# A third pair of key tiles in the second attention, and a norm's broadcast two projection steps later

## The chip, the cores and the metric

The kernel runs on one core of one Trainium2 chip. The metric is the device time of one execution in microseconds (us). The kernel before takes 2125.5 us in the median of three runs (2124.99 to 2128.76). A profiled execution, with the start and end of every instruction on each engine, took 2126.15 us.

The engines are named as in the profile: PE is TensorE (matmuls), PEld its weight loads, DVE is VectorE, ACT is ScalarE, POOL is GpSimd, SP is SyncE, which here only starts DMAs. Every engine works through its own instructions in a fixed order; an instruction waits until what it needs is done, and everything behind it on the same engine waits with it.

## What is computed

A trunk of two layers over 1024 tokens of width 1024, all in float32. Each layer is a token mixer with an attention of 12 heads (64 wide), beside it 4 heads that attend to 256 fixed memory tokens, then an output projection and a SwiGLU. Layer 0 mixes by windowed attention, layer 1 by attention over a neighbourhood on a grid.

```python
for i in range(DEPTH):                       # 2 layers
    h = rmsnorm(x, norm_mix[i])
    mk, mv = split(mem_n @ w_mem_kv[i])
    if i % 2 == 0:
        q, k, v, qm = split(h @ w_in_a)      # 12 query heads, 4 key/value heads
        y_tok = windowed_gqa(q, k, v, sink)
    else:
        q, k, v, qm = split(h @ w_in_b)      # 12 query, 12 key, 12 value heads
        y_tok = neighbourhood_attn(q, k, v, rpb)
    y_mem = memory_attn(qm, mk, mv)          # 4 heads
    x = x + concat([y_tok, y_mem]) @ w_out[i]
    h = rmsnorm(x, norm_ffn[i])
    x = x + (silu(h @ w_gate) * (h @ w_up)) @ w_down[i]
return rmsnorm(x, norm_final)
```

## The kernel before

Everything lies transposed, features on the 128 partitions and tokens along a row, in two column halves of 512 tokens (f = 0 and 1). To keep float32 accuracy, every operand is split into a high and a low part, and a product is three matmuls: high by high, high by low, low by high. A projection of 128 output features over one half is a sum of 8 steps (the 8 tiles of 128 input features) of 3 matmuls each, 24 matmuls of 128x512, named `mm`.

The split of a weight tile is a cast on ACT (the high part, line 106) and a subtraction on DVE or POOL (the low part, line 109). The tiles are `wf` for the first three units of a layer, then `wqk`, `wv` and `wqm` for units that make query and key, value, and memory query. Weights come by DMA from the queue of SP.

**The change of layers** is `first_dense`. While the down projection of layer 0 ends, it starts the three first units of layer 1 (24 matmuls each) on the first half, whose norm is done. Between the steps it pushes along the norm of the second half: squares, sums by matmul (`st`, line 213), a power of -1/2 (`nv` on DVE, `nr` on POOL), a diagonal matrix (`diag` on DVE, line 237), and a matmul with ones (`bc`, line 249) that spreads the factors over all partitions. Then eight times a scaling on DVE, a cast on ACT and a subtraction on DVE make the tiles `hT` of the second half, which the same three units need next. `Norm.split` has a number `lag`: so many calls pass between the diagonal and `bc`.

**The attention of a layer** (20 units and 16 heads in layer 1) runs units and heads at the same time. A head is worked in two halves of four query blocks. For each block a score product `S` (two matmuls, with the high and low part of the keys, KH and KL), the softmax on DVE, ACT and POOL, and per half the transposes of the four probability blocks `pT`, their split into `ph` and `pl`, and the products with the values, `O`. The heads' order is two memory heads, heads 0 to 5, the two other memory heads, heads 6 to 11. While a head's matmuls are put down, steps of the projections of later units are drawn in between (`pull`), as many as are due.

A unit `qk` of layer 1 makes the query tile `QS` of a head and its key tiles `KH` and `KL`. High parts of the keys are written by ACT and low parts by DVE straight out of the projection's PSUM bank, and two DMAs of SP (line 656) copy them to the other 64 partitions. The keys of a memory head (`mKH`, `mKL`, one pair for two heads) lie in tiles of the same ring. Before, the ring of layer 1 has 2 pairs and that of queries 3 tiles:

```python
nq = 4 if is_a else 3
Q[h] = k4("QS", nq, "QS")
K[i] = k4("KH", 2, "KH"), k4("KL", 2, "KL")
mk = k4("KH", 2, "mKH"), k4("KL", 2, "mKL")
```

The order in which each engine's instructions stand is not that of the code. A scheduler orders them when the program is built, by priority (the code's order) and by when an operand or a free tile is expected; a write to a ring that is full is put behind the last reader of the oldest tile. So the numbers of tiles and the address of each tile set the order and the waits. The tiles of a pool reuse the memory of the pools before it and wait for the last use there.

Of the kernel before, what the change touches and what calls it, by code (L numbers as in the profile page):

```python
# [41 lines left out]
def trunk_kernel(ctx: ExitStack, tc: tile.TileContext, a: dict, out: bass.AP):  # L42
# [68 lines left out]
    def load_w(src, tag="whl", bufs=3, eng=None, name="w", pool=wp, parts=1, raw=None):  # L111
        if raw is None:
            raw = raw_tile(f"{name}_raw")
            nc.sync.dma_start(raw, src)
        w = pool.tile([P, 2, D], F32R, tag=tag, name=name, bufs=bufs)
        for i in range(parts):
            c = slice(i * D // parts, (i + 1) * D // parts)
            hi(w[:, 0, c], raw[:, c])
            pieces = 4 if eng is nc.gpsimd else 1
            for j in range(pieces):  # L120
                n = D // parts // pieces
                cj = slice(i * D // parts + j * n, i * D // parts + (j + 1) * n)
                lo(w[:, 1, cj], raw[:, cj], w[:, 0, cj], eng)
        return w
# [9 lines left out]
    def steps(ps, w, h, order=range(NK), n=HS, start=True, stop=True):  # L134

        order = list(order)
        for i, k in enumerate(order):
            terms = three(wk(w, k), (h[k][:, 0, :n], h[k][:, 1, :n]))
            for j, (l, r) in enumerate(terms):
                nc.tensor.matmul(  # L140
                    ps[:, :n], l, r, start=start and i == 0 and j == 0,
                    stop=stop and i == len(order) - 1 and j == 2,
                )
            yield

    def run(g):
        for _ in g:
            pass
# [5 lines left out]
    def first_dense(layer, norm):  # L154

        pre = []
        src = a["w_in_b"]
        todo = (norm.add(x[k][1]) for k in range(len(norm.xs), NK))
        parts = norm.split(layer, hT[1], 6)
        for n, u in enumerate(FIRST[layer]):  # L160
            w = load_w(src[u], eng=nc.gpsimd, name="wf")
            wide[:] = True, (4, 2, 3)[n]
            ps = mm_tile()
            for i, _ in enumerate(steps(ps, w, hT[0])):
                if next(todo, 0) is not None and (n or i > 3):
                    next(parts, None)
            pre.append((w, ps))
        run(parts)
        return pre

    def mm_tile(name="mm"):

        wide[1] += 1
        if wide[0] and wide[1] % 5 > 2:
            return ps_s.tile([P, HS], F32, tag="S", name=name)
        if wide[0] and wide[1] % 5 == 0:
            return ps_t.tile([P, HS], F32, tag="T", name=name)
        return ps_mm.tile([P, HS], F32, tag="mm", name=name)
# [108 lines left out]
    with tc.tile_pool(name="mp", bufs=1, reuse_waits="tile") as mp:  # L287
# [60 lines left out]
        hT = [[None] * NK, [None] * NK]  # L348
# [12 lines left out]
        def total(norm, parts, n=D):  # L361

            both = []
            for t in parts:
                sq = mp.tile([P, D], F32, tag="sq", name="sq", bufs=2) if n == D else temp("sq")
                nc.scalar.activation(sq, t, AF.Square)
                both.append(sq)
                if len(both) > 1:
                    nc.vector.tensor_tensor(both[0], both[0], both.pop(), op=ALU.add)
                yield  # L370
            t = both[0]
            while n > norm.n:
                n //= 2
                nc.vector.tensor_tensor(t[:, :n], t[:, :n], t[:, n : 2 * n], op=ALU.add)
            norm.acc = [t[:, :n]]
            yield
# [8 lines left out]
        parts = total(norms[0], [xp[k, 0] for k in range(0, NK, 2)])  # L385
# [78 lines left out]
        for i in range(8):  # L464
# [11 lines left out]
            if i == 0:  # L476
                nc.scalar.copy(unit_scale, norms[0].scale())
                norms[1].xs = {k: x[k][1] for k in range(NK)}
                parts = total(norms[1], [xp[k, 1] for k in range(0, NK, 2)])
# [40 lines left out]
    for layer in range(2):  # L520
        is_a = layer == 0
        with tc.tile_pool(name=f"ap{layer}", bufs=1, reuse_waits="tile") as ap:
# [2 lines left out]
            wi = a["w_in_a"] if is_a else a["w_in_b"]  # L525
            n_tok = 10 if is_a else 18
            n_v = 8 if is_a else NH
            nq = 4 if is_a else 3


            def seen(ps):
# [6 lines left out]
            def placed(t, f):  # L538
                if is_a:
                    return t.rearrange("p (r f c) -> p f r c", f=2, c=32)[:, f]  # L540
                return t[:, f * HS : (f + 1) * HS].rearrange("p (s r c) -> p r s c", s=4, c=SC)

            def k4(tag, bufs, name):
                return ap.tile([P, S], F32R, tag=tag, bufs=bufs, name=name)

            def put_q(dst, f, ps, odd, order=True):

                rs = slice(HD, P) if odd else slice(0, HD)
                ot = slice(0, HD) if odd else slice(HD, P)
                if order:  # L550
                    src, h, l = seen(ps[rs]), placed(dst[rs], f), placed(dst[ot], f)
                    hi(h, src)
                    lo(l, src, h)
                else:
                    src, h, l = ps[rs], dst[rs, f * HS : (f + 1) * HS], dst[ot, f * HS : (f + 1) * HS]
                    nc.scalar.mul(h, src, SCALE)
                    nc.vector.scalar_tensor_tensor(
                        l, src, SCALE, h.bitcast(F32), op0=ALU.mult, op1=ALU.subtract
                    )

            def put_k(kh, kl, f, ps):
                rs = slice(HD, P)
                src, h, l = seen(ps[rs]), placed(kh[rs], f), placed(kl[rs], f)
                hi(h, src)
                lo(l, src, h)
# [14 lines left out]
            Q, K, V = {}, {}, {}  # L580

            class Unit:
# [21 lines left out]
                def open(self):  # L604
                    i = self.i
                    if self.kind == "qk":
                        h = 3 * i if is_a else i
                        Q[h] = k4("QS", nq, "QS")
                        K[i] = k4("KH", 2, "KH"), k4("KL", 2, "KL")
                        self.put = lambda f, ps: (put_q(Q[h], f, ps, False), put_k(*K[i], f, ps))  # L610
                    elif self.kind == "v":
                        V[2 * i], V[2 * i + 1] = (
                            ap.tile([P, 8, 2, HD], F32R, tag="V", bufs=4, name="V") for _ in range(2)
                        )
                        self.vt = ap.tile([P, S], F32, tag="vT", bufs=1, name="vT")
                        self.put = lambda f, ps: nc.scalar.copy(placed(self.vt, f), seen(ps))
                    else:
                        mem = self.kind == "qm"
                        hs = [("m", 2 * i), ("m", 2 * i + 1)] if mem else [3 * i + 1, 3 * i + 2]
                        for h in hs:  # L620
                            Q[h] = k4("QS", nq, "QS")
                        if mem:
                            mk = k4("KH", 2, "mKH"), k4("KL", 2, "mKL")
                            mv = ap.tile([P, 8, 2, HD], F32R, tag="V", bufs=4, name="mV")
                            K["m", i], V["m", i] = mk, mv
                            for j in range(2):
                                src = memk_d[layer, j][:, i * NM : (i + 1) * NM].rearrange(
                                    "(i p) k -> p i k", i=2
                                )
                                for rs in (slice(0, HD), slice(HD, P)):  # L630
                                    nc.sync.dma_start(
                                        mk[j][rs, :HS].rearrange("p (i k) -> p i k", i=2).bitcast(F32), src
                                    )
                            nc.sync.dma_start(
                                mv[:, :4].rearrange("p (b m) i d -> p b m (i d)", b=2).bitcast(F32),
                                memv_d[layer].rearrange("p (b m e) -> p b m e", b=2, m=NMH)[
                                    :, :, 2 * i : 2 * i + 2
                                ],
                            )
                        self.put = lambda f, ps: [  # L640
                            put_q(Q[h], f, ps, j == 1, order=not mem) for j, h in enumerate(hs)
                        ]
# [344 lines left out]
        with (  # L987
# [241 lines left out]
            for f in range(2):  # L1229
                for m in range(NK):  # L1230
# [15 lines left out]
                    if f == 1 and m == 0:  # L1246
                        norms[0].sums()
                        parts = norms[0].raw(2 + layer)
# [328 lines left out]
            parts = iter(())  # L1577
            hT = [[None] * NK, [None] * NK]
            for at_, (i, g) in enumerate(dorder):
# [28 lines left out]
                if i == 6 and g > 0:  # L1608
                    if g == 1:
                        parts = norms[0].split(1, hT[0], 1) if is_a else finish(norms[0])  # L1610
# [9 lines left out]
            if is_a:  # L1620
                pre = first_dense(1, norms[1])
            else:
                run(end)
                run(finish_end(quarter[1]))
# [88 lines left out]
```

## Time and profile before

| | before |
|---|---|
| median of three runs | 2125.5 us |
| profiled execution, its own time | 2126.15 us |
| span from first to last instruction | 2124.1 us |
| granted TensorE clock, mean | 0.998 |
| change of layers (first units of layer 1) | from about 1017 us |
| second attention | about 1066 to 1396 us |

A profile's time is that of one execution; the span lies between its first and last instruction, and 2.05 us lie around it. A row of a timeline has start, duration, engine, line, operation, output and input tiles, shape and count, and in square brackets the engine's idle time ahead of it with what ended it. The chain of waits follows the work that ended last back from the end: its rows have start, duration, engine, tile and line. In the timelines fp32 matmuls that take two passes (`st`, `bc`) count twice.

### The profile page before, as it was taken

The numbers are of one execution on the slowest core, as the hardware profiler recorded it, in microseconds if no ns is written. First come the engines' busy times: TensorE is split into PE (matmuls) and PEld (weight loads), VectorE is DVE, ScalarE is ACT, GpSimd is POOL, SyncE is SP. The second block draws the span as 40 slices with busy tenths as digits, with TensorE's granted clock in tenths as the row PEclk, the third lists the DMA queues.
The fourth block names the chain that finished last, engine by engine and source line by source line (L and its number), as shares of the span: only waits on it lengthen the run. The fifth ranks groups of instructions, "written<-read, shape, count | busy, mean of one in ns | idle before, by whom it ended". The sixth has DMA issues, their size and how long they took to land.

```text
span 2124.1 us, 29029 instructions
## 1 busy us (share of the span) xinstructions
PE 2094.9 (99%) x10316; PEld 1749.5 (82%) x10316; DVE 1521.0 (72%) x2477; ACT 1066.8 (50%) x2035; POOL 576.0 (27%) x614
## 2 busy tenths in 40 slices
PE   9999999999999999999999999999999999999998
PEld 7788888888888888888778888888788888888886
DVE  7687887787666666866765666667986666677675
ACT  6687775444434335344465666654443434344442
POOL 0344330234444430000233233203243444410000
PEclk9999999999999999999999999999999999999999
DMA  6421128332333227866232222275232323277662
GB/s 231 145 82 50 31 94 275 98 113 101 110 114 108 87 104 256 312 219 205 74 95 81 69 65 69 79 257 159 73 111 105 109 102 107 99 252 254 205 223 87
DMA packets 120913, 287.28 MB, mean 135 GB/s; under 512 B 12224, under 2 KB 20672, under 8 KB 120768
## 3 DMA queue, kind: packets, MB, share of 16 engines
q1 hardware_dynamic: 112880, 271.63, 37.9%
q10 hardware_dynamic: 7888, 13.79, 1.7%
q8 instruction: 82, 1.34, 0.3%
q14 instruction: 63, 0.52, 0.1%
HBM read 210.40 MB, written 68.94 MB: 132 GB/s over the span
## 4 chain that ended last, share of the span: by engine, by line
PE 90%; DVE 4%; ACT 2%; issue 1%; DMA 1%; POOL 1%; ACTq 0%; DVEq 0%; SPq 0%; POOLq 0%
PE X L1078 16%; PE Y L1078 16%; PE mm L140 15%; PE X L1509 11%; PE Y L1509 8%; PE po L140 8%; PE O L786 3%; PE S L723 3%; PE pT L766 3%; PE X L1160 2%; PE Y L1160 2%; PE mm L426 1%; DMA wd_kept<-in_w_dn 1%; DVE pl L109 0%; PE bc L249 0%
## 5 line engine op out<-in xcount | busy, mean ns | idle before, releaser
L1078 PE MATMUL Y<-hB,wgu 128*128 128x512 f32 x1056 | 255.6, 391 | 0.8 <-ACT c L1098 0.8
L1078 PE MATMUL X<-hB,wgu 128*128 128x512 f32 x1056 | 255.0, 391 | 0.0
L1509 PE MATMUL X<-hB,wd 128*128 128x512 f32 (+1 forms) x1092 | 243.8, 383 | 0.9 <-DVE x L1473 0.9
L109 DVE TENSOR_TENSOR wgu<-wS,wgu 128x1024 fp32r<-128x1024 f32 (+1 forms) x124 | 152.9, 1233 | 121.7 <-ACT wgu L106 121.6
L1509 PEld LDWEIGHTS X<-hB,wd 128*128 128x128 f32 x1092 | 200.1, 188 | 41.9 <-issue 2.2
L1078 PEld LDWEIGHTS Y<-hB,wgu 128*128 128x128 f32 x1056 | 196.7, 188 | 43.4 <-ACT c L1098 1.6
L1078 PEld LDWEIGHTS X<-hB,wgu 128*128 128x128 f32 x1056 | 195.8, 188 | 40.2 <-ACT g L1095 0.4
L751 POOL TENSOR_SCALAR p<-p,stat 128x384 f32<-128x384 f32 (+1 forms) x256 | 139.3, 563 | 317.7 <-DVE stat L748 223.1
L140 PE MATMUL mm<-hT,wqk 128*128 128x512 f32 x672 | 197.5, 404 | 1.5 <-DVE KL L109 1.5
L106 ACT CAST wgu<-wS 128x1024 fp32r<-128x1024 f32 (+1 forms) x124 | 114.2, 923 | 149.9 <-POOL wS L1035 124.5
L140 PE MATMUL po<-yT,wo 128*128 128x512 f32 x768 | 185.6, 394 | 0.0
L1509 PE MATMUL Y<-hB,wd 128*128 128x512 f32 x792 | 180.7, 389 | 0.1
L1509 PEld LDWEIGHTS Y<-hB,wd 128*128 128x128 f32 x792 | 148.5, 188 | 31.7 <-DVE x L1473 0.5
L234 POOL TENSOR_TENSOR nr<-nv,neg_half 128x4 f32<-128x4 f32 (+1 forms) x12 | 13.4, 1116 | 586.0 <-DVE nv L233 582.1
L140 PEld LDWEIGHTS po<-yT,wo 128*128 128x128 f32 x768 | 142.5, 188 | 29.9 <-issue 1.0
L1078 PE MATMUL X<-hT,wgu 128*128 128x512 f32 x624 | 150.2, 391 | 0.0
L106 ACT CAST hB<-b_raw 128x512 fp32r<-128x512 f32 x154 | 89.5, 618 | 113.5 <-DMA b_raw<-b_d 94.5
L1035 POOL TENSOR_TENSOR wS<-wgu_raw 128x512 f32<-128x512 f32 x44 | 60.9, 1384 | 294.6 <-DVE wgu L109 294.6
L1078 PEld LDWEIGHTS X<-hT,wgu 128*128 128x128 f32 x624 | 117.0, 188 | 26.2
L738 ACT ACTIVATE p<-p,stat 128x256 f32<-128x256 f32 (+1 forms) x192 | 112.5, 587 | 51.5 <-DVE stat L734 49.5
L109 DVE TENSOR_TENSOR pl<-pT,ph 128x384 fp32r<-128x384 f32 (+1 forms) x256 | 118.5, 492 | 18.4 <-ACT ph L106 15.3
L109 DVE TENSOR_TENSOR hB<-b_raw,hB 128x512 fp32r<-128x512 f32 x154 | 99.8, 686 | 42.8 <-ACT hB L106 42.4
(208 smaller groups left out, 4230.6 us busy)
## 6 DMA issues: line engine op xcount, KB each, us to landing
wgu_raw<-in_w_gu SPq DMA_DIRECT2D x92, 512.0 KB
wd_raw<-in_w_dn SPq DMA_DIRECT2D x70, 512.0 KB
b_raw<-b_d SPq DMA_DIRECT2D x70, 512.0 KB
b_d<-c SPq DMA_DIRECT2D x88, 256.0 KB
b_d<-t SPq DMA_DIRECT2D x66, 256.0 KB
wo_raw<-in_w_out SPq DMA_DIRECT2D x32, 512.0 KB
xr_d<-x ACTq DMA_DIRECT2D x32, 256.0 KB
xr<-xr_d SPq DMA_DIRECT2D x16, 512.0 KB
```

The source lines that it names most:

```text
L106: nc.scalar.copy(dst, src)
L109: (eng or nc.vector).tensor_tensor(dst, src, h.bitcast(F32), op=ALU.subtract)
L140: nc.tensor.matmul(ps[:, :n], l, r, start=start and i == 0 and j == 0, stop=stop and i == len(order) - 1 and j == 2,)
L723: nc.tensor.matmul(s_[:, :n], Q[self.h][:, qb * P : (qb + 1) * P], k, start=j == 0, stop=j == 1)
L738: nc.scalar.activation(p[:, :n], p[:, :n], AF.Exp, bias=m1, scale=-1.0, accum_out=s1)
L751: nc.gpsimd.tensor_scalar(p[:, :n], p[:, :n], ri[:, i : i + 1], 1.0, op0=ALU.mult, op1=ALU.mult)
L766: nc.tensor.transpose(tr[:, j * P : (j + 1) * P], p[:, j * P : (j + 1) * P], ident)
L786: nc.tensor.matmul(o[:, c0 : c0 + w * P], self.value(j), t[:, s0 : s0 + w].rearrange("p j q -> p (j q)"), start=j == js[0] and t is self.p ...
L1035: sub = lambda o, p_, q_: nc.gpsimd.tensor_tensor(o, p_, q_, op=ALU.subtract)
L1078: nc.tensor.matmul(ps, l, r, start=n in (0, 1, 3, 6) and k == 0 and i == 0, stop=k == 3 and i == 2, skip_group_check=True,)
L1160: nc.tensor.matmul(bank[:, at : at + h2], l, r, start=start and k == 0 and i == 0, stop=stop and k == 1 and i == 2, skip_group_check=True,)
L1509: nc.tensor.matmul(bank[:, c], l, r, start=i in (0, 1, 3, 6) and p == 0 and n == 0, stop=p == HF - 1 and n == 2, skip_group_check=True,)
```

## The change

In `first_dense` the number of calls that pass before the second half's broadcast goes from 6 to 8. In layer 1's attention the ring of queries has 4 tiles in place of 3, and that of keys 3 pairs (KH and KL) in place of 2; layer 0 keeps 4 and 2. This is 12 KB more per partition. The new line moves every line number behind 528 up by one.

```diff
@@ first_dense
-        parts = norm.split(layer, hT[1], 6)
+        parts = norm.split(layer, hT[1], 8)
@@ attention of a layer
-            nq = 4 if is_a else 3
+            nq = 4
+            nk = 2 if is_a else 3
@@ Unit.open, unit "qk"
-                        K[i] = k4("KH", 2, "KH"), k4("KL", 2, "KL")
+                        K[i] = k4("KH", nk, "KH"), k4("KL", nk, "KL")
@@ Unit.open, unit "qm"
-                            mk = k4("KH", 2, "mKH"), k4("KL", 2, "mKL")
+                            mk = k4("KH", nk, "mKH"), k4("KL", nk, "mKL")
```

On PE at the change of layers stood, before:

```order
L140 MATMUL mm<-hT,wf 128x512 x29
L213 MATMUL st<-inv_d,sq 128x1 x4
L140 MATMUL mm<-hT,wf 128x512 x6
L249 MATMUL bc<-diag,ones 128x512
L140 MATMUL mm<-hT,wf 128x512 x109
```

and now stands:

```order
L140 MATMUL mm<-hT,wf 128x512 x29
L213 MATMUL st<-inv_d,sq 128x1 x4
L140 MATMUL mm<-hT,wf 128x512 x10
L249 MATMUL bc<-diag,ones 128x512
L140 MATMUL mm<-hT,wf 128x512 x105
```

The broadcast moves behind four matmuls of the projections; what stands ahead of the sums (st) is the same.

On PE in the memory heads of layer 1, behind the first half's O products (the projections are those of the unit for head 2), stood before:

```order
L786 MATMUL O<-ph,mV 128x512
L766 MATMUL pT<-ident,p 128x128
L786 MATMUL O<-pl,mV 128x512
L723 MATMUL S<-mKH,QS 128x256
L723 MATMUL S<-mKL,QS 128x256
L786 MATMUL O<-ph,mV 128x512
L786 MATMUL O<-pl,mV 128x512
L766 MATMUL pT<-ident,p 128x128
L723 MATMUL S<-mKH,QS 128x256
L723 MATMUL S<-mKL,QS 128x256
L766 MATMUL pT<-ident,p 128x128
L140 MATMUL mm<-hT,wqk 128x512 x33
```

and now, from the first half's O products on:

```order
L787 MATMUL O<-ph,mV 128x512
L787 MATMUL O<-pl,mV 128x512
L140 MATMUL mm<-hT,wqk 128x512 x3
L787 MATMUL O<-ph,mV 128x512
L787 MATMUL O<-pl,mV 128x512
L140 MATMUL mm<-hT,wqk 128x512 x3
L767 MATMUL pT<-ident,p 128x128 x4
L140 MATMUL mm<-hT,wqk 128x512 x3
L767 MATMUL pT<-ident,p 128x128 x2
L140 MATMUL mm<-hT,wqk 128x512 x6
```

The projections of this unit, 33 matmuls in a row before, are drawn between the transposes and scores of the memory heads. The block of 36 matmuls of `wv` behind it dissolves in the same way. From about 1119 us of the trace of before on, PE's order is the same.

On the queue of SP stood at the start of the second attention, from the third early weight load on:

```order
L114 DMA wv_raw<-in_w_in_b 128x1024
L675 DMA braw<-bias_d 128x384
L114 DMA wqk_raw<-in_w_in_b 128x1024
L656 DMA KH<-KH 64x1024
L656 DMA KL<-KL 64x1024
```

and now:

```order
L114 DMA wv_raw<-in_w_in_b 128x1024
L657 DMA KH<-KH 64x1024
L657 DMA KL<-KL 64x1024
L114 DMA wqk_raw<-in_w_in_b 128x1024
L676 DMA braw<-bias_d 128x384
```

The copies of head 1's keys stand ahead of a bias load and a weight load that they followed.

## The prediction

> **What bounds the kernel now.** The page first: its head, and the busy time of each engine.
>
> ```profile
> span 2124.1 us, 29029 instructions
> PE 2094.9 (99%) x10316; PEld 1749.5 (82%) x10316; DVE 1521.0 (72%) x2477; ACT 1066.8 (50%) x2035; POOL 576.0 (27%) x614
> ```
>
> TensorE sets the end: it is busy for 2094.9 of 2124.1 us, so only 29 us of idle can be won in the whole kernel, and a moved instruction is worth something only where TensorE stands still. The change touches one stretch, from the change of layers at about 1017 us into the second attention. What TensorE waits for between 1017 and 1130 us, from the view of waits (line waited for, total, times, longest):
>
> ```profile
> PE mm L140 <- DVE KL L109: 2.1, 2, 1.5
> PE pT L766 <- DVE pl L109: 1.6, 2, 0.9
> PE bc L249 <- DVE diag L237: 1.1, 1, 1.1
> PE O L786 <- ACT ph L106: 0.2, 1, 0.2
> ```
>
> That is 5.0 us in all: 1.1 at the norm's broadcast (bc), 3.9 in the attention. The rows of TensorE's timeline with a wait behind them place the 3.9:
>
> ```profile
> 1085.14 0.96 PE L766 MATMUL pT<-ident,p 128*128 128x128 f32 x5 [0.86 <-DVE pl L109]
> 1089.88 7.78 PE L140 MATMUL mm<-hT,wqk 128*128 128x512 f32 x33 [1.55 <-DVE KL L109]
> 1105.64 0.74 PE L766 MATMUL pT<-ident,p 128*128 128x128 f32 x4 [0.72 <-DVE pl L109]
> 1106.53 0.51 PE L786 MATMUL O<-ph,mV 128*128 128x512 f32 x1 [0.15 <-ACT ph L106]
> 1110.47 8.46 PE L140 MATMUL mm<-hT,wv 128*128 128x512 f32 x36 [0.58 <-DVE KL L109]
> ```
>
> Read the 33 and the 36 projection matmuls as the sign of the shortage. Two projections stood still, since their results could not be read out: the key tiles had no free pair. So TensorE ran through scores and transposes alone, faster than VectorE could serve them, waited, and then did the projections in one block. The table of windows (span; then busy us of PE, PEld, DVE, ACT, POOL) prices the two places against an undisturbed piece of the same attention:
>
> ```profile
> core 0: us, PE busy (x) PEld busy (x) DVE busy (x) ACT busy (x) POOL busy (x), PEclk, DMA share, GB/s
> 1066.50:1118.90 52.40, 48.47 (x253) 39.67 (x251) 32.40 (x81) 33.92 (x94) 19.93 (x32) 1.00 0.29 80
> 1083.40:1089.90 6.50, 4.03 (x25) 2.75 (x23) 5.71 (x14) 6.18 (x16) 3.00 (x5) 1.00 0.24 49
> 1103.10:1110.50 7.40, 5.95 (x38) 4.63 (x37) 6.24 (x18) 7.22 (x18) 2.14 (x4) 1.00 0.01 2
> 1130.00:1380.00 250.00, 249.30 (x1355) 211.12 (x1353) 162.69 (x387) 156.96 (x386) 75.32 (x119) 1.00 0.24 71
> ```
>
> **Part 1: the broadcast later.** Nothing is added. In the order bc moves behind four more matmuls (x6 becomes x10). The chain of waits there (start, us, what):
>
> ```profile
> 1030.51 6.57 PE mm L140 x29
> 1037.08 0.97 PE st L213 x8
> 1038.08 0.17 DVE nv L233
> 1038.32 1.02 POOL nr L234
> 1039.36 1.22 DVE diag L237
> 1040.62 1.12 PE bc L249 x2
> 1041.75 24.76 PE mm L140 x109
> ```
>
> From the end of st (1038.06) to bc (1040.62) the chain over VectorE and GpSimd takes 2.56 us, and TensorE has six matmuls to fill it: 24.76/109 = 0.227 us each, 1.4 us. Four more fill 0.9 us. The chain itself doesn't move, so bc starts at the same moment and TensorE is 0.9 us ahead in the projections: **-0.9**. Behind bc stand VectorE's eight scaled tiles (hT), which now have 33 matmuls of cover in place of 37:
>
> ```profile
> 1043.77 1.89 DVE L109 TENSOR_TENSOR hT<-h,hT 128x512 fp32r<-128x512 f32 x3
> 1050.78 1.35 DVE L109 TENSOR_TENSOR hT<-h,hT 128x512 fp32r<-128x512 f32 x2
> ```
>
> The first three are there by 1045.66, the last by 1052.13. TensorE wants the first at 1041.75 + 33 x 0.227 = 1049.2 and the eighth 21 matmuls (4.8 us) later, at 1054.0: 1.9 us of cover on the last. Bounds: 0 (if hT turns out late by as much) and 1.1, the whole row.
>
> **Part 2: the third pair of key tiles and the fourth query tile.** No instruction is added or removed; the order changes. The 33-matmul block dissolves into threes and sixes between scores and transposes, and the weight block of 36 likewise. So at 1083.4 and 1103.1 TensorE has projections to do while VectorE works. What that is worth has two readings. By the idle rows: 0.86 + 1.55 + 0.72 + 0.15 + 0.58 = 3.9 us. By weight loads: undisturbed attention loads for 211.12/250 = 0.844 of the time, so 2.75 us are 3.3 us of work in 6.5, and 4.63 are 5.5 in 7.4: 3.2 + 1.9 = 5.1 us lost; the whole 52.4 us give 39.67/0.844 = 47.0, so 5.4. I take **-5.2**, since the busy time of a matmul that stands alone holds more than its slot (0.51 for one O above, 0.93 for four in a row below). Bounds: 2.1 (only the two KL waits go, the transposes wait as before) and 5.4.
>
> The Trainium skill, "Perfetto Trace Analysis", section "Identifying the Most-Contended Engine", calls matmul busy time no good measure, because matmuls are pipelined, and names the busy share of weight loads in its place. Busy time here would give a sum of 0.9 + 3.9, weight loads 0.9 + 5.2. The trace bears the page out as far as it goes: the window from 1083.4 is 62% busy by PE and only 42% by PEld.
>
> **New waits.** The thinnest place that I found in the new order: the fourth pair of transposes in the third memory half waits for VectorE's subtraction (pl) of the first pair, and the split of a weight tile (wqk) stands ahead of that one. From the end of the second half-projection, with these rows for the pieces (TensorE from the chain, the others from their timelines):
>
> ```profile
> 1078.96 0.22 PE pT L766 x2
> 1079.18 0.24 PE S L723 x2
> 1079.42 0.70 PE mm L140 x3
> 1082.22 0.93 PE O L786 x4
> 1082.32 0.57 ACT L106 CAST QS<-mm 64x512 fp32r<-64x512 f32 x1
> 1082.78 0.47 ACT L730 ACTIVATE p<-S,stat 128x256 f32<-128x256 f32 x1
> 1084.77 1.07 ACT L106 CAST wqk<-wqk_raw 128x1024 fp32r<-128x1024 f32 x1
> 1083.98 0.68 DVE L807 TENSOR_TENSOR y<-O,yt 64x512 f32<-64x512 f32 x1 [0.18 <-ACT yt L796]
> 1086.82 1.22 DVE L109 TENSOR_TENSOR wqk<-wqk_raw,wqk 128x1024 fp32r<-128x1024 f32 x1
> 1089.13 1.30 DVE L109 TENSOR_TENSOR KL<-mm,KH 64x512 fp32r<-64x512 f32 x2 [0.43 <-ACT KH L106]
> 1084.59 1.07 DVE L109 TENSOR_TENSOR pl<-pT,ph 128x256 fp32r<-128x256 f32 x3
> ```
>
> ScalarE 0.57 + 0.47 + 1.07 and VectorE 1.22 + 0.65 + 0.68 + 0.36 make 5.0 us, with some 0.2 of handing over 5.2. TensorE in between has a score pair 0.24, four O 0.93, fifteen projections 3.5, six transposes 0.66 and half a score pair 0.12: 5.45. So 0.2 us of cover; without it the price is the wait it was before, 0.86. I put **+0.3** for this and its like; bounds 0 and 1.6 (0.86 + 0.72, both transposes' waits back).
>
> **Moved queue entries.** On SP the copies of a key pair (KH, KL) come ahead of the next weight load and the bias load (braw), since they no longer wait for the memory heads' last scores. By the program's waits, the memory keys' load is no longer held by GpSimd's split of wf, and the residual's first load (x) after the attention now waits for the last softmax scaling and a transpose after it:
>
> ```profile
> 1041.18 1.27 SPq L631 DMA_DIRECT2D mKH<-memk_d  x2
> 1390.74 2.02 SPq L1018 DMA_DIRECT2D x<-x_d  x4
> 1388.22 2.16 POOL L751 TENSOR_SCALAR p<-p,stat 128x384 f32<-128x384 f32 x4 [2.56 <-DVE stat L748]
> 1401.72 0.68 DVE L1241 TENSOR_TENSOR x<-po,x 128x512 f32<-128x512 f32 x1
> ```
>
> The first is earlier than its users (scores, after 1066) by 25 us already. The x load's new releaser ends by 1390.4 and its transpose follows within about a microsecond, and x is wanted at 1401.72: 10 us of cover, cost nothing; if that were gone, each microsecond late costs one. Queued behind x are a weight and y loads of the same stage.
>
> **The sum.** Against the profiled execution's own 2126.15 us (span 2124.1 and 2.05 around it): 2126.15 - 0.9 - 5.2 + 0.3 = 2120.35. That execution lies 0.65 above the median of the runs, 2125.5; on that scale it is 2119.7. I forecast **2120.0**. After the attention TensorE runs full, so what is won stays won.
>
> **Rivals.**
> - *Only the idle counts.* The busy time of the two windows is work that takes as long anyway: 0.9 + 3.9 - 0.3 = 4.5, time 2121.3 between the two scales. For it: PE busy rows say so. Against it: PEld at 42%.
> - *The waits move.* VectorE and ScalarE are 5.71 and 6.18 us busy in the 6.5 us window; with projections in between, each of the memory halves still meets a late pl or key read: 0.86 + 1.55 + 0.86 come back, 6.1 - 3.3 = 2.8, time 2123.0. For it: the thin cover above, with a weight split in each half. Against it: over the whole 52.4 us VectorE is busy 62%, and over 47 us it would be 69%.
> - *The change doesn't do what it says:* the projections wait for their result banks for another reason (the query tiles, the weight), and the third pair is not used early. Then 0.9 is left: 2124.9. Against it: both KL rows name the key read alone.
> - *Slower.* The splits of weight tiles, with TensorE further ahead, delay pl in the rest of the attention too: 12 further units (20, less 3 done at the start and 5 whose splits fall in the window), each with one split of 1.22 on VectorE. At the mean of the two long waits, 1.2 us, that is 14.4 - 6.1 = 8.3 more, 2134; it decides from 0.5 us a unit on. Against it: the window 1130 to 1380 holds the same splits and TensorE idles 0.7 of 250 us.
>
> **Chances.** Forecast 0.58 (gains of 4.6 to 6.5, times 2119 to 2121.5), idle alone 0.15, moved waits 0.16, no early use 0.07, slower 0.04. About 0.2%, 4.25 us, is what a measurement of this kernel can tell from no change. All of the first and two thirds of the second lie beyond it: faster 0.68; the rest of the second, the third and fourth: same 0.28; slower 0.04. The range runs from the largest bounds, 1.1 + 5.4 off the median and 1 us for the spread of runs, 2118, to the third case with the same spread, 2124.0. It leaves out the fourth and the last.
>
> **What would show it.** Right: the bc row waits under 0.3 us; no block of 33 or 36 projections, and no KL wait in TensorE's waits between 1017 and 1125; the point where 36 weight matmuls ended (1118.9) comes 5 to 6 us sooner, with PEld near 0.84. Wrong: new rows of pT behind pl in that stretch (third case), a KL row that stays (fourth), pT waits all through 1120 to 1380 (last), or PE's idle gone and the span still shorter by 4.5 alone (second).

## The result, and the profile after

| | before | after |
|---|---|---|
| median of 16 runs each | 2125.46 us | 2121.33 us |
| profiled execution, its own time | 2126.15 us | 2121.35 us |
| its span | 2124.1 us | 2119.5 us |

The ratio is 0.9981 (95% interval 0.9974 to 0.9988), a gain of 4.1 us with 2.6 to 5.5 us as its interval. The point itself, 0.19%, is just short of the 0.2% that the prediction named as the least that can be told; the interval reaches past it on one side. The kernels were timed against each other twice more (below): gains of 5.4 and 5.0 us. Over all executions of the three timings, 35 of the changed kernel and 61 of the kernel before, the medians are 2120.9 and 2126.0, a gain of 5.1 us (4.5 to 5.4 by resampling), 0.24%.

Where it came from. First TensorE's waits between 1017 and 1130 us in the profile of after; the same view of before had four rows with 5.0 us.

```profile
PE bc L249 <- DVE diag L237: 0.2, 1, 0.2
```

The waits behind KL, pl and ph are all gone, and bc's went from 1.1 to 0.2. In the attention up to 1130 us no block of 33 or 36 projections is left; the longest is 16 in a row, at its start. Then TensorE's own timeline. Three of its rows can serve as marks in both kernels, because the instructions there are the same in both: the sums of squares (st), the first transposes of the values (vtr) after them, and the next block of eight, which lies behind the point where both orders are the same again. Before:

```profile
1036.99 1.05 PE L213 MATMUL st<-inv_d,sq 128*128 128x1 f32 x8
1066.34 0.60 PE L573 MATMUL vtr<-ident,vT 128*128 128x128 f32 x4
1123.43 1.26 PE L573 MATMUL vtr<-ident,vT 128*128 128x128 f32 x8
```

After:

```profile
1035.83 1.05 PE L213 MATMUL st<-inv_d,sq 128*128 128x1 f32 x8
1039.48 1.12 PE L249 MATMUL bc<-diag,ones 128*128 128x512 f32 x2 [0.18 <-DVE diag L237]
1064.26 0.60 PE L574 MATMUL vtr<-ident,vT 128*128 128x128 f32 x4
1116.87 1.26 PE L574 MATMUL vtr<-ident,vT 128*128 128x128 f32 x8
```

The marks cut out two stretches. The first, with bc in it, takes 1066.34 - 1036.99 = 29.35 us before and 28.43 after. The second, the attention up to where the orders meet, takes 57.09 before and 52.61 after. That is 0.92 and 4.48 us, 5.40 in all. The windows of the two stretches, before (span; then busy us of PE, PEld, DVE, ACT, POOL):

```profile
1036.99:1066.34 29.35, 28.26 (x126) 22.83 (x126) 19.57 (x28) 11.87 (x19) 4.14 (x6) 1.00 0.36 109
1066.34:1123.43 57.09, 53.16 (x277) 43.83 (x275) 33.71 (x86) 35.38 (x99) 21.36 (x35) 1.00 0.27 75
```

And after:

```profile
1035.83:1064.26 28.43, 28.25 (x127) 22.85 (x127) 18.36 (x27) 10.85 (x18) 3.94 (x6) 1.00 0.26 78
1064.26:1116.87 52.61, 52.52 (x276) 43.21 (x275) 35.94 (x87) 37.39 (x100) 20.85 (x35) 1.00 0.27 82
```

In the second stretch TensorE stood idle for 57.09 - 53.16 = 3.93 us before and for 0.09 after. Its busy time shrank as well, by 0.64. Weight loads fill 82.1% of the stretch (43.21/52.61) where they filled 76.8%.

The profile of after was 1.16 us ahead at st already, before anything is changed, and so 6.56 us ahead behind the second stretch; at the end 4.6 were left. Of the 1.16, 0.8 is a single wait in the first attention, of transposes behind ScalarE's vT: 1.6 us in the profile of before and in that of e9, 0.7 to 0.8 in the ten others, so no part of the change. One of the places where some of the 6.56 was lost again is a wait just before the last down projection (columns as in a timeline, the wait in brackets). Before:

```profile
1891.72 0.98 PE L1160 MATMUL Y<-hT,wgu 128*128 128x256 f32 x6 [0.45 <-DVE c L1188]
```

After:

```profile
1885.89 0.97 PE L1161 MATMUL Y<-hT,wgu 128*128 128x256 f32 x6 [1.41 <-DVE c L1189]
```

The other lies behind the last issue of an output: 3.75 us to the end of the span before, 5.11 after. Whether these belong to the change was the first question to the experiments.

### The profile page after: what moved, and what is told of

It reads as the page before. It is cut to its first block, busy times and chain, and to the rows that moved or that the text cites. A ratio compares the mean times of both kernels' runs of the same rounds, so it can differ in the third digit from the quotient of the medians.

```text
span 2119.5 us, 29023 instructions
## 1 busy us (share of the span) xinstructions
PE 2094.4 (99%) x10316; PEld 1750.1 (83%) x10316; DVE 1522.0 (72%) x2477; ACT 1067.0 (50%) x2035; POOL 575.1 (27%) x614
## 4 chain that ended last, share of the span: by engine, by line
PE 91%; DVE 3%; ACT 2%; DMA 1%; issue 1%; POOL 1%; DVEq 0%; ACTq 0%; SPq 0%; POOLq 0%
PE X L1079 17%; PE Y L1079 16%; PE mm L140 15%; PE X L1510 11%; PE Y L1510 8%; PE po L140 8%; PE O L787 3%; PE S L724 3%; PE pT L767 3%; PE X L1161 2%; PE Y L1161 2%; PE mm L426 1%; DMA wd_kept<-in_w_dn 1%; PE bc L249 0%; POOL wS L1036 0%
## 5 line engine op out<-in xcount | busy, mean ns | idle before, releaser
L1079 PE MATMUL Y<-hT,wgu 128*128 128x512 f32 x528 | 129.9, 391 | 0.0
```

What stands on the lines that cost most here:

```text
L1079: nc.tensor.matmul(ps, l, r, start=n in (0, 1, 3, 6) and k == 0 and i == 0, stop=k == 3 and i == 2, skip_group_check=True,)
```

## The experiments

The table has every profile, read at the same marks. "Late load" is the stretch from the first row of the last q4h products to the first matmul of the last down projection, where the wait above lies; "end" is the time from the last output's issue to the end of the span. Time is the median against the median of before timed beside it; the kernels without one have a single execution.

| kernel | first stretch | second | sum | late load | end | time against before |
|---|---|---|---|---|---|---|
| before | 29.35 | 57.09 | 86.44 | 7.05 | 3.75 | |
| eight steps alone (e1) | 28.46 | 57.42 | 85.88 | 7.77 | 3.72 | -0.3 |
| fourth query alone (e5) | 29.35 | 57.09 | 86.44 | 7.90 | 3.80 | |
| pools alone (e2) | 29.35 | 52.37 | 81.72 | 7.71 | 4.48 | -4.8 |
| three keys, three queries, eight steps (e3) | 28.42 | 52.86 | 81.28 | 6.93 | 3.75 | -5.3 |
| after | 28.43 | 52.61 | 81.04 | 7.99 | 5.11 | -4.1 |
| after again (e4) | 28.46 | 52.62 | 81.08 | 8.08 | 4.34 | -5.4 |
| after again (e10) | 28.46 | 52.70 | 81.16 | 8.19 | 4.31 | -5.0 |
| nine steps (e6) | 27.99 | 53.04 | 81.03 | 7.95 | 4.38 | |
| split on GpSimd (e7) | 28.45 | 52.53 | 80.98 | 7.71 | 5.15 | |
| three pairs in both (e8) | 28.45 | 52.66 | 81.11 | 6.86 | 4.03 | |
| late weight on GpSimd (e9) | 28.44 | 52.69 | 81.13 | 6.35 | 3.77 | -7.7 |

In the three profiles of the changed kernel the stretches repeat within 0.1 us, while whole runs of one kernel timed together differ by 1 to 8 us. So the parts of the change are read from the stretches, and the times only say whether what is won there arrives.

**The broadcast later, alone (e1).** The kernel before with `parts = norm.split(layer, hT[1], 8)`.

> Only the first part: the norm's broadcast eight projection steps behind in place of six, the key and query pools as before. If the sum of the prediction holds part by part: the wait of bc falls from 1.1 to about 0.2 us, the stretch from the first projections of the second half to the transposes of the values takes 35.1 us in place of 36.0, the attention behind it stays at 52.4 us with its blocks of 33 and 36 projections, and the time is 0.9 us under before. If instead the time won there is only moved into the attention (TensorE reaches the same late key read 0.9 us sooner and waits for it 0.9 us longer): the attention's stretch takes 53.3 us, KL waits of 3.0 in place of 2.1, and no change in the time.

The first stretch went as the sum has it, 0.89 us shorter. The second became 0.33 longer with no wait more. So 0.56 is left; the measured 0.3 cannot be told from it nor from nothing (ratio 0.9992 to 1.0009). The second theory named the right place and the wrong size: a third is handed back, not all. Where, the chain of waits shows. Before, at the first transposes:

```profile
1066.51 0.44 PE vtr L573 x4
1066.94 0.48 PE S L723 x4
1067.42 0.23 PE mm L140
1067.65 0.44 PE vtr L573 x4
```

With the broadcast two steps later:

```profile
1065.91 0.44 PE vtr L573 x4
1066.35 0.23 PE S L723 x2
...
1066.59 0.65 PE vtr L573 x4
```

The second four transposes read the second half of vT, which ScalarE copies from the last projection's bank. Before, four score matmuls and a projection stood between and covered the copy; now there are two score matmuls, and the transposes take 0.65 us in place of 0.44. The copy, before and then with the broadcast two steps later:

```profile
1066.54 0.59 ACT L616 COPY vT<-mm 128x512 f32<-128x512 f32 x1 [2.00 <-PE mm L140]
```

```profile
1065.95 0.59 ACT L616 COPY vT<-mm 128x512 f32<-128x512 f32 x1 [3.30 <-PE mm L140]
```

Now it ends at 1066.54, and the transposes begin at 1066.59. The copy itself did not come late: in both kernels it starts 0.20 us behind the first of the transposes (1066.34 before, 1065.75 now). What changed is the order. The scheduler put one of the two score pairs and the projection behind the second four transposes, so there is less between the two fours to cover the copy. The rest of the 0.33 lies in single score pairs behind it (0.34 for 0.23, for one).

**The pools alone (e2).** The changed kernel with `norm.split(layer, hT[1], 6)`.

> Only the second part: a third pair of key tiles and a fourth query tile, the broadcast six steps behind as before. By the trace of the changed kernel: the stretch to the transposes stays at 36.0 us, the attention's stretch takes 48.0 us in place of 52.4, no KL wait there. Time: 4.5 us under before, if all that is won there reaches the end; 3.5 us under before, if a microsecond of it is given back in the last feed-forward block, where the changed kernel's profile shows a wait of 1.4 us on a late load of the down projection's weights that the profile of before has at 0.45 us.

The second stretch is 4.72 us shorter, the first is unchanged, and there is no wait behind KL or pl. Its window:

```profile
1066.01:1118.38 52.37, 52.27 (x276) 43.24 (x275) 34.71 (x86) 36.49 (x99) 20.96 (x35) 1.00 0.28 83
```

Idle time went from 3.93 to 0.10, which is 3.83, and busy time from 53.16 to 52.27, which is 0.89. The measured 4.8 us agrees with 4.5 or 4.7 all arriving, and the interval of the ratio (0.9971 to 0.9989, 2.3 to 6.2 us) does not exclude 3.5. In the whole change the second stretch is 0.24 to 0.33 longer than here: the later broadcast hands back the same here as it does alone.

**Three key pairs with three query tiles (e3).** In the changed kernel `nq = 4 if is_a else 3`.

> The changed kernel with three query tiles in place of four, so the third key pair and the late broadcast alone. If the key tiles alone held the projections back: the attention's stretch 48.0 us as in the changed kernel, time 5 us under before. If the query tile is needed as well, a part of the projections stands behind scores again: one or two waits of 0.3 to 0.9 us come back, the stretch takes 48.5 to 50 us, time 3 to 4.5 us under before.

No wait comes back. The second stretch is 52.86, 0.2 us more than in the three profiles of the changed kernel. So the key tiles carry nearly all of it.

**The fourth query tile alone (e5).** In the kernel before `nq = 4` and nothing else.

> The kernel before with the fourth query tile alone: two key pairs, the broadcast six steps behind. If the key pairs alone hold the projections: nothing moves, the two stretches 29.35 and 57.1 us (from the sums of squares to the first transposes of the values, and from there to the second), with TensorE's waits of 2.1 us behind KL and 1.6 us behind pl. If the query tiles held them too: a shorter second stretch, the block of 33 projections before the 1.55 us wait smaller.

TensorE's waits between 1030 and 1120 us:

```profile
PE mm L140 <- DVE KL L109: 2.1, 2, 1.5
PE pT L766 <- DVE pl L109: 1.6, 2, 0.9
```

They, and the two smaller ones behind them, are the rows of before, and both stretches are the same to 0.01 us. TensorE's order with this tile is that of the kernel before, row by row. The query tile does nothing while there are two key pairs, and is worth 0.2 us beside a third.

**The changed kernel again (e4, e10).**

> The changed kernel once more, nothing altered. Its first profile was 5.4 us shorter over the two changed stretches (0.93 and 4.46), 6.55 us ahead behind them with an offset of 1.16 us that it had before it reached them, and 4.6 us shorter at the end: 1.0 us went at a late load before the last down projection and 1.35 us behind the last issue of an output. If these three are chance of one execution: the two stretches come out at 35.1 and 48.0 us again, the wait at the late load near 0.5 us and the end behind the last issue near 3.8 us in this profile, or other values again, and the median over the runs is 4 to 5.5 us under before. If they belong to the change: 1.4 us and 5.1 us again, and the median 4.1 us or less under before.

> The changed kernel beside it on the same chip, nothing altered. If the spread behind the changed stretches is chance: the two stretches 28.4 and 52.6 us, the end anywhere within a microsecond and a half of the earlier profiles, and the median 4 to 5.5 us under before. If part of the gain is given back by the change itself: 4.1 us or less again.

The stretches repeat and the medians are 5.4 and 5.0 us under before, as the first theory has it. The stretch with the late load does not follow that theory: it takes 8.1 and 8.2 us again (waits of 1.48 and 1.59 us), so that is not one execution's chance. But the kernel of e1, with none of the pools, has 7.77, that of e5 7.90, and that of e3, with a third key pair, 6.93. There are two groups: in before, e3 and e8 ScalarE's copy of c waits for TensorE's own product and TensorE then waits 0.26 to 0.45 us; in the others, but for e9, the copy stands behind a cast that waits 0.8 to 1.5 us for its load, and TensorE waits 1.1 to 1.6. Kernels with and without a third key pair are in both, so it does not go with the change; what puts a kernel into one of them is open. The end behind the last issue stayed over 4 us in all three profiles of the changed kernel; more on it in the last section.

The sum over a profile is a balance of such places. The three profiles of the changed kernel are 1.2 to 1.5 us ahead of the one of before at st, win 5.3 to 5.4 in the two stretches, and lose 0.9 to 1.1 at the late load and 0.6 to 1.4 at the end. With one profile of before, nothing tells how much of the gain and the losses outside the stretches belongs to that one execution. That the medians come so near to the 5.3 is in part luck.

**Nine steps (e6).** `norm.split(layer, hT[1], 9)` in the changed kernel.

> The changed kernel with the broadcast nine projection steps behind in place of eight, that is behind thirteen matmuls in place of ten. If only the chain over VectorE and GpSimd sets bc's wait: 0.2 becomes 0, the first stretch 28.2 us in place of 28.43, the scaled tiles still in time (the last with 1.2 us of cover by the prediction's reckoning), the second stretch 52.6 us again or up to 0.2 more. If the scaled tiles come late instead: a new wait of projections behind hT in the first stretch, and no gain over 28.43.

Neither came as put down. The wait of bc is gone and the first stretch is 0.44 us shorter; the scaled tiles are not late; and the second stretch is 0.42 longer. The sum is 81.03 against 81.04 to 81.16. The second four transposes take 0.66 us as with eight steps, so it is not lost there. Counted in matmuls from st, the kernel is 0.44 us ahead of the changed kernel at the first transposes of the values, still 0.41 after 168 matmuls and only 0.08 after 184. The order between differs once more, and the chain has these rows there:

```profile
1073.53 0.48 PE S L724 x2
...
1074.70 0.35 PE pT L767 x2
...
1075.30 0.36 PE S L724 x2
```

Two score matmuls take 0.24 us elsewhere in this chain and two transposes 0.22, so these three rows hold 0.5 us more than that; what they wait for, the trace does not name. In this one profile, what the ninth step takes off one stretch it puts on the other.

**The split that was to make pl late (e7).** In the changed kernel, one weight tile's low part on GpSimd:

```diff
-self.src, eng=nc.gpsimd if is_a else None, name=f"w{self.kind}", raw=self.raw
+self.src, eng=nc.gpsimd if is_a or (self.kind, self.i) == ("qk", 3) else None,
+name=f"w{self.kind}", raw=self.raw
```

> The changed kernel with the low part of one weight tile, the fourth head's query and key weights, made by GpSimd and not by VectorE. It is the split of 1.23 us that stands ahead of pl in VectorE's queue in the third memory half, where the fourth pair of transposes takes 0.41 us in place of 0.22. If that split makes pl late, as the prediction has it: 0.22 there, the second stretch 52.4 us in place of 52.61. If pl waits for ScalarE's ph or TensorE's own transposes: 0.41 stays. If GpSimd's four pieces of about 0.74 us hold up the scaling of p: transposes wait for p, and the stretch is up to a microsecond longer.

In the changed kernel VectorE's queue in the third memory half is this:

```profile
1082.58 1.23 DVE L109 TENSOR_TENSOR wqk<-wqk_raw,wqk 128x1024 fp32r<-128x1024 f32 x1 [0.51 <-ACT wqk L106]
1083.84 0.69 DVE L109 TENSOR_TENSOR KL<-mm,KH 64x512 fp32r<-64x512 f32 x1
1084.57 0.68 DVE L808 TENSOR_TENSOR y<-O,yt 64x512 f32<-64x512 f32 x1
1085.17 1.07 DVE L109 TENSOR_TENSOR pl<-pT,ph 128x256 fp32r<-128x256 f32 x3
1085.73 0.41 PE L767 MATMUL pT<-ident,p 128*128 128x128 f32 x2
```

The last row is TensorE's, the fourth pair of transposes. With the split on GpSimd:

```profile
1082.92 0.69 DVE L109 TENSOR_TENSOR KL<-mm,KH 64x512 fp32r<-64x512 f32 x1 [1.11 <-ACT KH L106]
1083.65 0.68 DVE L809 TENSOR_TENSOR y<-O,yt 64x512 f32<-64x512 f32 x1
1084.26 1.07 DVE L109 TENSOR_TENSOR pl<-pT,ph 128x256 fp32r<-128x256 f32 x3
1084.81 0.41 PE L768 MATMUL pT<-ident,p 128*128 128x128 f32 x2
```

Measured from st of its own kernel, pl starts at 49.34 us with the split ahead of it and at 48.70 without, 0.64 sooner. The fourth transposes are put two projections earlier in the order, still take 0.41 us, and the stretch is 0.08 us shorter. That does not clear pl. A row of three pl holds three of 0.41 us each that overlap, so the first ends at 1085.58 here and at 1084.67 there, and the pair begins 0.15 and 0.14 us behind that end. The same distance stands in the kernel before, where the profile names pl as what ended the wait: first pl until 1085.00, transposes from 1085.14. So the pair waits for pl in both kernels, as the prediction said; the new order only moved it up to where the earlier pl ends. With the split gone and the order moved, TensorE wins a tenth of a microsecond.

**A third pair in the first attention (e8).** `nk = 3` for both layers, and `nq = 3 if is_a else 4`: in the first attention the third pair is paid for with the fourth query tile.

> The changed kernel with a third key pair in the first attention too, paid for by its fourth query tile. In the first attention TensorE waits 0.57 us once for KL and 3.0 us in eight places for pl. If the rule carries over (a projection that stands before scores gives TensorE work while VectorE subtracts): the KL wait goes and pl waits shrink, 0.6 to 2 us won between 60 and 395 us. If the queries bind there: new waits, the first attention as long or longer.

TensorE's waits between 60 and 397 us, in the profile of after and then in this one:

```profile
PE pT L767 <- DVE pl L109: 3.0, 7, 0.8
...
PE mm L140 <- DVE KL L109: 0.6, 1, 0.6
PE S L724 <- ACT p L731: 0.3, 1, 0.3
```

```profile
PE pT L767 <- DVE pl L109: 2.5, 7, 0.8
PE S L724 <- ACT p L731: 1.0, 2, 0.8
...
PE mm L140 <- DVE KL L109: 0.6, 1, 0.6
PE mm L140 <- DVE QS L558: 0.5, 1, 0.5
```

The KL wait stays, 0.5 us less behind pl stands against 0.7 us more of scores behind p and a new wait of 0.5 for a query tile. Nothing is won; the changed stretches of the second attention are the same. Two things changed at once here, so this run does not tell what a third pair would be worth beside four query tiles.

**The late load (e9).** In the changed kernel the second weight tile of each down projection goes wholly to GpSimd, which is idle there:

```diff
-hi(two(w[:, 0], n), src)
-lo(two(w[:, 1], n), src, two(w[:, 0], n))
+if (i, g) == (0, 1):
+    nc.gpsimd.tensor_copy(two(w[:, 0], n), src)
+    lo(two(w[:, 1], n), src, two(w[:, 0], n), nc.gpsimd)
+else:
+    hi(two(w[:, 0], n), src)
+    lo(two(w[:, 1], n), src, two(w[:, 0], n))
```

> The changed kernel with the second weight tile of each down projection split (high and low part) by idle GpSimd, where ScalarE and VectorE did it. In nine profiles, with and without the change, the stretch from the last 'q4h' product to the first down-projection matmul took 6.86 to 8.08 us, because ScalarE stands in that split waiting for a load and the copy of c queues behind it. If that late load, and not the change, takes back about a microsecond: the wait of Y behind c is under 0.2 us, this stretch takes 6.3 to 6.5 us, and the time is 0.5 to 1.5 us under the changed kernel. If TensorE only meets the same saturated transfers at the next place: the stretch shrinks, but the down projection behind it grows by as much, and the time is the changed kernel's.

In the third profile of the changed kernel, ScalarE stands for 1.49 us waiting for the weight's load, and its copy of c queues behind the cast. VectorE's half of the split waits for that cast, and the c for which TensorE waits queues behind that:

```profile
1883.08 1.05 ACT L106 CAST wd<-wd_kept 128x1024 fp32r<-128x1024 f32 x1 [1.49 <-DMA wd_kept<-in_w_dn]
1884.03 0.58 ACT L1104 COPY c<-X 128x512 f32<-128x512 f32 x1
1884.16 1.23 DVE L109 TENSOR_TENSOR wd<-wd_kept,wd 128x1024 fp32r<-128x1024 f32 x1 [1.47 <-ACT wd L106]
1885.30 0.41 DVE L1189 TENSOR_TENSOR c<-c,Y 128x256 f32<-128x256 f32 x1
1885.77 0.98 PE L1161 MATMUL Y<-hT,wgu 128*128 128x256 f32 x6 [1.59 <-DVE c L1189]
```

With the tile on GpSimd, TensorE there, and GpSimd in its place:

```profile
1886.08 0.88 PE L1161 MATMUL X<-q4h,wgu 128*128 128x256 f32 x6
1886.80 0.88 PE L1161 MATMUL Y<-hT,wgu 128*128 128x256 f32 x6
1885.55 1.04 POOL L1423 CAST wd<-wd_kept 128x1024 fp32r<-128x1024 f32 x1 [13.91 <-DMA wd_kept<-in_w_dn]
```

The wait is gone, the stretch takes 6.35 us in place of 8.19, and the down projection behind it is no longer (218.5 us from its first matmul to the last bc, 218.4 to 218.9 in the changed kernel). The median is 2118.24 (5 runs) against 2120.89 of the changed kernel on the same chip (8 runs) and 2125.93 of before: ratio to before 0.9961 (0.9949 to 0.9974). This version beats both. The 2.65 us against the changed kernel are more than expected; 1.84 in the late load and the shorter end (3.77 for 4.31) would make 2.4, and resampling gives 0.3 to 3.5. The profiled execution is the slowest of the five (2120.59 us) and shows none of this in its time: it fell 2 us behind between 73 and 80 us, where the wait of transposes behind vT was 0.8 us longer and the mean granted clock from 74 to 80 us was 0.72 (1.00 in the third profile of the changed kernel). The edit lies elsewhere.

## Why the prediction came out as it did

The predicted 2120.0 was 1.3 us under the median of the first timing, inside its range, and 0.9 under the median over all three. The first timing alone does not decide for the forecast: its gain of 4.1 us is less than the 4.6 to 6.5 that were forecast, and its 2121.33 is the very time that the rival "only the idle counts" gives, 2121.3. The other two timings and the stretches decide. By its steps:

- *Part 1, -0.9.* The size in its own stretch was right (0.89 to 0.93 in all kernels with eight steps). The step that failed is the cover of what stands behind bc: it reckoned only with the scaled tiles, which were in time even at nine steps, and took the order behind them as unchanged. The scheduler moved a score pair and a projection 25 us on, and the transposes of the values then stood uncovered behind ScalarE's copy of vT. Net: 0.56 alone, 0.56 to 0.68 on top of the pools.
- *Part 2, -5.2.* Right in place and mechanism: three key pairs dissolve the blocks of 33 and 36, and all five waits go. The size is 4.72, 0.5 less than the term. Of the two readings, the idle rows gave 3.9, and 3.83 of idle time did go; weight loads gave 5.1 to 5.4. The reading by weight loads was mis-sized because it took the undisturbed 0.844 as what this stretch would reach. It reached 43.24/52.37 = 0.826; at 0.844 the same loads would have taken 51.2 us, 1.1 less. The loads' own busy time fell by 0.6, which gives back 0.7 at that share, and that the two nearly cancel is luck. Truth lay 0.8 above the one reading and 0.5 below the other, so matmul busy time did hold about 0.9 us of stalling, and a share from another stretch was no exact price either. The Trainium skill, "Perfetto Trace Analysis", section "Identifying the Most-Contended Engine", calls matmul busy time no good measure; it does not speak of stalls in it.
- *New waits, +0.3.* The thin place was where it was said to be, and for the cause given, pl. The 0.2 us of cover was not there: the pair begins 0.14 to 0.16 us behind the end of pl in all three profiles of the changed kernel, the distance at which it waited before, and takes 0.41 us in place of 0.22. So 0.2 us of the 0.3 was paid, in the stretch's time and not in the view of waits, since the score matmul ahead still counts as busy (0.28 us, where its like follow each other every 0.12).
- *Moved queue entries, nothing.* From the second vtr mark to the last transposes of the values the changed kernel takes 229.64 to 229.68 us in three profiles, before 229.61, and no new wait stands at the residual.
- *What is won stays won.* On the whole yes: 5.3 to 5.4 us in the stretches, 5.1 in the medians. But "TensorE runs full" after the attention was too much said; before the down projection it waits 0.3 to 1.6 us behind c (not at all in e9), and part of the spread between kernels is made there and at the end.
- *Rivals.* "The waits move" came only as the 0.2 us above, with no new pT row among the waits, and "slower" did not come: the rest of the attention is as long as before. "The change doesn't do what it says" is refuted for the key tiles, and would have been true of the query tile alone. "Only the idle counts" was near in its sum (4.5) and right about the idle, but 0.9 of busy time went too with the same matmuls (e2; 0.6 in the whole change).

Predicted for the two stretches together: -5.8. Measured: -5.3 to -5.4. The second part with its new waits was put at -4.9 and came to -4.72 alone; the later broadcast then handed back 0.2 to 0.3, for which no term stood.

## What to carry to other kernels

When the engine that sets the end shows long blocks of one kind of work with waits just ahead of them, look for the ring of tiles that lets that work start: one more tile can spread the block into the gaps, and here its worth lay between the idle time of the gaps and what a weight-load share of the neighbouring stretch would give. Moving one instruction can change the scheduler's order far behind it, so compare the whole order of the busiest engine on both sides, and look for products of other engines that have lost what covered them, not only at the first user. And before moving more matmuls about, see whether an instruction that waits for a load stands in a queue ahead of one that TensorE needs: moving it to an idle engine won more here (2.6 us, 0.3 to 3.5) than the first part did (about 0.6).

## What was not expected of the hardware

The end of the program. Behind the last issue of an output the span goes on for 3.7 to 5.2 us. The DMA queues from that moment to the end of the span (packets, MB, share), first before, then after:

```profile
q1 hardware_dynamic: 479, 0.44, 35.1%
q10 hardware_dynamic: 416, 0.39, 30.6%
```

```profile
q1 hardware_dynamic: 481, 0.44, 26.2%
q10 hardware_dynamic: 416, 0.39, 22.2%
q14 instruction: 1, 0.01, 0.4%
```

In the changed kernel a packet of a queue that carries instructions falls among the last packets of the output. It is so in all three of its profiles and in those of e2, e6 and e7, all with an end of 4.3 to 5.2 us; in the six profiles without such a packet there (before, e1, e3, e5, e8, e9) the end takes 3.7 to 4.0. The records of the packet give it 0.31 us, so it alone does not make up the difference. The Trainium skill, "DMA: Bandwidth & Descriptors", section "Why a DMA increments its semaphore by 16 and not by 1", says that each of the DMA engines ends its share with a write of its own that lands after its data; a packet ahead of one of these would hold up the whole. The order of the records goes with that where the end is longest: in the first profile of the changed kernel the instruction packet starts at 2117.02 and one last small packet of the output at 2117.32, right behind it, and so in e7 (ends of 5.1 and 5.2 us). In the other four the last small packet starts no later than the instruction packet, and the end takes 4.3 to 4.5. That the instruction packet causes the longer end was not tried on its own, and stays open.
